# Where the operands of TensorE start within 128 bytes of SBUF: moving them, and joining two pools of slots

## The chip, the core and the metric

The kernel runs on one core of a Trainium2 chip. The metric is the device time of one execution in microseconds (us). Before the change it is 1717.04 us, the median of three runs (1714.14 to 1718.41).

The engines of a core run side by side and in order, each from its own queue: TensorE (PE in the profile; its weight loads stand apart as PEld), VectorE (DVE), ScalarE (ACT), GpSimd (POOL), and SyncE (SP), which here issues every DMA. TensorE reads both operands of a matmul from SBUF: the stationary one is loaded into the array (LDWEIGHTS), then the moving one is streamed through it. Results go to PSUM.

## The reference

Two layers (`DEPTH` 2) over a sequence of 512 rows of width 1024. Each layer projects x, runs four token mixers on 256 columns each, merges them under gates, projects and normalises, and then does a SwiGLU feed-forward network (FFN) of width 2816:

```
for l in range(DEPTH):
    h = x @ w_in[l]
    ...
    o_ret = _retention(rq, rk, rv, rg)
    o_att = _chunk_attention(aq, ak, av, att_rel_bias[l])
    o_gla = _gla(gq, gk, gv, gr, ga, gla_w_a[l], gla_b_a[l])
    o_s5 = _s5(su, ...)
    for bi in range(N_BRANCH):        # summed over the four branches
        gate = sigmoid(x @ w_gate[l, bi] + b_gate[l, bi])
        mixed = mixed + gate * (branches[bi] @ w_branch[l, bi])
    x = _layer_norm(DEEPNORM_ALPHA * x + mixed @ w_out[l], ...)
    ffn = (silu(x @ w_ffn_gate[l]) * (x @ w_ffn_up[l])) @ w_ffn_down[l]
    x = _layer_norm(DEEPNORM_ALPHA * x + ffn, ...)
```

All of it is float32.

## The kernel before

**Numbers.** A float32 operand of a matmul is split into a high part h (ScalarE casts it to float32r) and a low part l (VectorE subtracts h). A product takes three matmuls: h·h, h·l, l·h. So TensorE does three times the plain work, 11,596 matmuls in all, of up to 512 moving columns each.

**What lies where.** x^T stays in SBUF as XH and XL, eight slices of 128 rows by 512 columns each. A tile of weights of 128 by 1024 comes by DMA into `wr` and is split into `wh` and `wl` (`wload`, L312; pool `wp`, three buffers of each). Everything else of 128 by 512 lives in slots (`slot`, L161) of 2048 bytes per partition: 41 of tag "a", 7 of "sg" and 8 of "acc" in the pool `ap`, and 12 of tag "w" in the pool `ap2`. `ap2` lies 64 bytes further than a multiple of the slot's size behind `ap`, because of a tile of 16 floats between them (L148 to L150). A tag's slots are handed out in turn, and a tile waits until the last reader of the slot's former tile is done.

**The stages of a layer.** First come the projections that all branches need (`gemm_n`, tiles gn, with x^T stationary and the weights moving; then su, aq, ak by `gemm_t`, with the weights stationary and x^T moving, 256 columns at a time, tiles of 48 matmuls). Then the mixers run, as generators that `run` (L984) interleaves by the clock of a planner (`Pace`, L51): attention, retention (rq, rk, rg), gla (gq, gr) and s5, and as filler `gate_stream` (L917), which alternates gate tiles (`pg`, 48 matmuls of x^T against w_gate) and branch tiles (`pb`, 6 matmuls of 512 columns, the branch br moving against its weights bw stationary). Then `proj_ln` (L444) multiplies the merged rows (mh, ml, stationary) by w_out (moving, tiles pj) and normalises. The FFN makes 44 tiles `pg` of x^T against w_gate and w_up, and `proj_ln` again multiplies their results (gh, gl, stationary) by w_down (moving, tiles pj). In `proj_ln` all k but the last two take their weights by `wload`; the last two by `wload_s` (L327) into slots `wsh`, `wsl`. Of the 22 tiles gh and gl of the FFN, f = 0 to 6 and 13 to 21 lie in `ap`, f = 7 to 12 in `ap2`.

**The s5 mixer** (L770) works through eight blocks j. A block's input u is fetched by DMA (`skr`), cast by ScalarE to `stk`; its matrix is split into `sbs` (once for two blocks, `split_b`, L778: a cast by ScalarE, a subtraction by VectorE); two matmuls `sv` read both; a chain on VectorE turns them into states (m1 to m4 are named sm); `xr` and `xi` are split from those; six matmuls `sy` take them one block later, against `cpd`. At the end comes `sg`, a small product with `swg`.

**Order.** The calls stand in the order in which the generators run, and the tile framework then orders the instructions of each engine by priority and by its own estimates; when a slot comes free is part of that. On the chip each engine takes its queue strictly in order.

**Where the operands start,** as the built program has them (bytes past a multiple of 128; matmul slices within a tile start at multiples of 512 bytes but for a few of gn):

| tiles | before | after |
|---|---|---|
| XH, XL | 0 | 0 |
| wh, wl (and wr) | 64 | 64 |
| constants ct (identity for transposes) | 0 | 64 |
| slots of `ap`: br, mh, gh (16 of 22), wsh, stk, xr, xi, v, ... | 0 | 64 |
| slots of `ap2`: bw, sbs, cpd, swg, gh (f = 7 to 12) | 64 | 64 (in `ap`) |

Of the kernel before, what the change touches and what calls it, by code (L numbers as in the profile page):

```python
# [10 lines left out]
F32 = mybir.dt.float32  # L11
F32R = mybir.dt.float32r
# [4 lines left out]
P = 128  # L17
S = 512
# [18 lines left out]

BUFS = {"a": 41, "sg": 7, "acc": 8, "w": 12}

# [89 lines left out]
def trunk_kernel(ctx: ExitStack, tc: tile.TileContext, xn, xt, wt, w2, wbr, wo, wgu, wdn,  # L134
# [6 lines left out]
    def pool(name, bufs, **kw):  # L141
        return ctx.enter_context(tc.tile_pool(name=name, bufs=bufs, **kw))

    cp = pool("cp", 1)
    wp = pool("wp", 3)
    sm = pool("sm", 2)
    ap_ = pool("ap", 53)
    pad = pool("pad", 1)  # L148
    ap2 = pool("ap2", 12)
    pad.tile([P, 16], F32, name="pad")  # L150
    psm = pool("psm", 3, space=bass.MemoryType.PSUM)
    psx = pool("psx", 5, space=bass.MemoryType.PSUM)
    dr = pool("dr", 1, space=bass.MemoryType.DRAM)
# [3 lines left out]
    def nm(s):  # L157
        uid[0] += 1
        return f"{s}{uid[0]}"

    def slot(s, dt=F32, tag="a"):  # L161
        n = nm(s)
        return (ap2 if tag == "w" else ap_).tile([P, 512], dt, tag=tag, name=n, bufs=BUFS[tag])

    def mm_ps(s):
        n = nm(s)
        x = psm.tile([P, 512], F32, tag="mm", name=n)
        pace.ring("mm", 3, x)
        return x

    def mx_ps(s):
        n = nm(s)
        x = psx.tile([P, 512], F32, tag="mx", name=n)
        pace.ring("mx", 5, x)
        return x

    def split(h, l, src):
        A.copy(h, src)
        V.tensor_tensor(l, src, h.bitcast(F32), ALU.subtract)

    def split_slots(s, src, tags=("a", "a")):
        h, l = slot(s + "h", F32R, tags[0]), slot(s + "l", F32R, tags[1])
        split(h, l, src)
        return h, l

    def three(pairs):

        (ah, al), (bh, bl) = pairs
        return ((ah, bh), (ah, bl), (al, bh))


    XH = cp.tile([P, 8, S], F32R, name="XH")
    XL = cp.tile([P, 8, S], F32R, name="XL")

    def load_x(k):
        r = slot("xr")
        SP.dma_start(r, xt[:, k, :])
        with tc.high_priority():
            split(XH[:, k, :], XL[:, k, :], r)

# [138 lines left out]
    def gemm_t(src, s, late=None):  # L339

        return gemm_ts([src], s, late)[0]

    def gemm_ts(srcs, s, late=None):
        wl = [wload(x) for x in srcs]
        pss = [mm_ps(s) for _ in srcs]
        for (t0, t1) in ((0, 256), (256, S)):
            for i, ((h, l), ps) in enumerate(zip(wl, pss)):
                if late and t0 == 0 and i == len(wl) - 1:
                    late()
                n = 0  # L350
                for w, xx in ((h, XH), (h, XL), (l, XH)):
                    for k in range(8):
# [5 lines left out]
    def gemm_n(srcs, width, pre=None, late=None):  # L358
# [4 lines left out]
        def prod(c, t):  # L363
            h, l = ws[c]
            for kk in range(2):
                k = 2 * c + kk
                for j, (xx, w) in enumerate(((XH, h), (XL, h), (XH, l))):
                    T.matmul(pss[t][:, :width], xx[:, k, P * t:P * t + P],
# [16 lines left out]
    def layer_norm(l, w_, xh, pss, gt, bt, t, last):  # L385
# [30 lines left out]
        def rest():  # L416
# [15 lines left out]
            for h in range(2):  # L432
                split(XH[:, 4 * h:4 * h + 4, P * t:P * t + P], XL[:, 4 * h:4 * h + 4, P * t:P * t + P],
                      xf[h].rearrange("p (k c) -> p k c", c=P))
# [335 lines left out]
    def s5(l, s5c, uspr, br):  # L770

        bst = {}
# [3 lines left out]
            SP.dma_start(r[0:96, :], sb[l, :, 512 * c:512 * c + 512])  # L776

        def split_b(c):  # L778
            r, b = bst[c], slot("sbs", F32R, "w")
            A.copy(b[0:96, :], r[0:96, :])  # L780
            V.tensor_tensor(b[64:96, :], r[64:96, :], b[64:96, :].bitcast(F32), ALU.subtract)
            bst[c] = b
# [32 lines left out]

        def inputs(j):
            u0, g0 = 32 * (j % 4), j // 4
            cpd = slot("cpd", F32R, "w")
            G.memset(cpd.bitcast(F32), 0.0)
            cp4 = cpd.rearrange("p (s i c) -> p s i c", s=2, i=2)  # L820
            csrc = cc.rearrange("p (i j c) -> p i j c", i=2, c=32)[:, :, j]
            split(cp4[:, 0, :, u0:u0 + 32], cp4[:, 1, :, u0:u0 + 32], csrc)
            vv = []
            u = ust.pop(j)
            for i in range(2):
                ps = mx_ps("sv")
                c0 = 256 * (j % 2) + P * i
                T.matmul(ps, bst[j // 2][0:96, c0:c0 + P], u[0:96, :], start=True, stop=True)
                vv.append(ps)
            er, ei = tabs[j]  # L830
            m1, m2, m3, m4 = (slot("sm") for _ in range(4))
            V.tensor_tensor(m1, vv[0], er, ALU.mult)
            V.tensor_tensor(m4, vv[0], ei, ALU.mult)
            V.tensor_tensor(m2, vv[1], ei, ALU.mult)
            V.tensor_tensor(m3, vv[1], er, ALU.mult)
            V.tensor_tensor(m1, m1, m2, ALU.add)
            V.tensor_tensor(m3, m3, m4, ALU.subtract)
            return cp4, m1, m2, m3, m4
# [40 lines left out]
        for j in range(8 + LAG):  # L879
# [9 lines left out]
            if j == 6:  # L889
                wg = slot("swg")  # L890
# [2 lines left out]
                yield [*xs[j - LAG][1], *xs[j - LAG][2]]  # L893
                outputs(j - LAG)
        yield [wg]
        wgh = split_slots("swg", wg, ("w", "w"))
        yield [*wgh, *yg[0][1], *yg[1][1]]
        for p in range(2):
            ps = mx_ps("sg")
            n = 0  # L900
# [16 lines left out]
    def gate_stream(l, order, brs, mix):  # L917


        sgs, bws, acc = {}, {}, [None] * 8  # L920

        def gate(bi, i):
            pg = gemm_t(wt[l, 13 + 8 * bi + i], "pg")
            sgs[bi, i] = slot("sg", tag="sg")
            A.activation(sgs[bi, i], pg, AF.Tanh, bias=hb[:, l, 8 * bi + i:8 * bi + i + 1], scale=0.5)

        def load(bi, c):
            bws[bi, c] = slot("bwr")
            SP.dma_start(bws[bi, c], wbr[l, bi, c])

        def branch(bi, i, first, last):
            sg = sgs.pop((bi, i))
            pb = mm_ps("pb")
            n = 0
            for k in range(2):
                for a, b in three((bws[bi, i // 2], brs[bi][k])):
                    c0 = 256 * (i % 2) + P * k
                    T.matmul(pb, a[:, c0:c0 + P], b, start=(n == 0), stop=(n == 5))
                    n += 1
            if first:  # L940
                acc[i] = slot("acc", tag="acc")
                V.scalar_tensor_tensor(acc[i], sg, 1.0, pb, ALU.add, ALU.mult)
            else:
                V.scalar_tensor_tensor(sg, sg, 1.0, pb, ALU.add, ALU.mult)
                (V if last else G).tensor_tensor(acc[i], acc[i], sg, ALU.add)
            if last:

                h, l_ = slot("mh", F32R), slot("ml", F32R)
                A.activation(h, acc[i], AF.Copy, scale=0.5)
                V.scalar_tensor_tensor(l_, acc[i], 0.5, h.bitcast(F32), ALU.mult, ALU.subtract)  # L950
                mix.append((h, l_))

        todo = [(bi, i) for bi in order for i in range(8)]
        ng = nb = nl = ns = 0

        def inputs_at():
            x = brs[todo[nb][0]]
            return None if x[0] is None or x[1] is None else pace.ready([*x[0], *x[1]])

        def can():  # L960
            return 0.0 if ng < len(todo) and ng - nb < CAP else inputs_at()

        while nb < len(todo):
            yield can
            at = inputs_at()
            more = ng < len(todo) and ng - nb < CAP
            if ng - nb >= 2 and at is not None and at <= pace.at["T"] or not more:
                branch(*todo[nb], nb < 8, nb >= 24)
                nb += 1
            else:  # L970
                gate(*todo[ng])
                ng += 1

            while ns < min(nl, (nb + 6) // 2):
                c = todo[2 * ns][0], todo[2 * ns][1] // 2
                if pace.when(bws[c]) > pace.at["T"] and ns > nb // 2:
                    break
                bws[c] = split_slots("bw", bws[c], ("w", "w"))
                ns += 1
            while nl < min(len(todo), nb + 6) // 2:  # L980
                load(todo[2 * nl][0], todo[2 * nl][1] // 2)
                nl += 1
# [23 lines left out]
    for l in range(L):  # L1006
# [73 lines left out]
        for f in range(NF):  # L1080
            if f > 0:
                ps += [gemm_t(wgu[l, i], "pg") for i in range(max(3, 2 * f), 2 * f + 2)]
            pg, pu = ps[2 * f:2 * f + 2]
            if f == 1:
                rows()
            s = slot("fs")
            A.activation(s, pg, AF.Silu)
            V.tensor_tensor(s, s, pu, ALU.mult)
            h, l_ = split_slots("g", s, ("acc", "acc") if f < 4 else ("sg", "sg") if f < 7 else
                                ("w", "w") if f < 13 else ("a", "a"))  # L1090
            ghs.append(h)
            gls.append(l_)
            if l + 1 < L and f == 0:
                s5c = s5_constants(l + 1)
            if l + 1 < L and f % 2 == 0 and 4 <= f < 20:
                j = f // 2 - 2
                for i, x in enumerate(s5_table(j, s5c[3])):
                    SP.dma_start(esp[j, i], x)
# [141 lines left out]
```

## Time and profile before

| | |
|---|---|
| time, median of 3 runs | 1717.04 us |
| time of the profiled execution | 1721.47 us |
| its span, first to last instruction | 1719.4 us |
| granted TensorE clock, mean of the span | 0.979 of full speed |
| busy: PE, PEld, DVE, ACT, POOL | 96%, 89%, 59%, 36%, 21% |
| matmuls | 11,596 |

The times below are microseconds from the start of the span. Layer 0 runs its mixers from about 67 to 459, w_out to 487, the FFN to about 858; layer 1 follows with its mixers from 905 to 1299, w_out to 1327, and the FFN to the end. A matmul's own duration in the trace (about 390 ns for 512 columns) is its passage through a pipeline: the next one starts before it ends. What a stream of matmuls costs is read from the distance of their starts. In the timeline equal neighbours are merged: a row gives the start of the first, the time to the end of the last, and their count.

### The profile page before, as it was taken

What the parts mean: (1) busy time and instruction counts of PE and PEld (TensorE: products, weight loads), DVE (VectorE), ACT (ScalarE), POOL (GpSimd) and SP (SyncE); (2) the same over time, 40 slices, a digit from 0 to 9 for tenths busy, and PEclk for the clock granted to TensorE, in tenths of its full rate; (3) what the DMA queues carried; (4) which work ended last, traced back from release to release, by engine and by line L of the source; (5) the groups of instructions that cost most, each with busy time, mean ns of one, the idle gap of its engine ahead of it and who ended that gap; (6) DMA issues with size and microseconds to landing.
All of it is one profiled execution on the core that took longest, in us unless ns stands there. A gap on an engine that the chain in (4) does not pass through costs nothing. (4 is left out here: it accounts for less than half of the span.)

```text
span 1719.4 us, 27810 instructions
## 1 busy us (share of the span) xinstructions
PE 1650.6 (96%) x11596; PEld 1526.8 (89%) x11596; DVE 1005.9 (59%) x1473; ACT 613.0 (36%) x1012; POOL 353.4 (21%) x363
## 2 busy tenths in 40 slices
PE   8998999789999999999999999999899999999997
PEld 7988998679889999998889889988898899999886
DVE  4667579998577443332374765699965833333226
ACT  4443442233343222221253545433332522222112
POOL 0602015642018931000052000121200600000002
PEclk9998999899999999999999999999999999999999
DMA  5522322222432433322317332233424232332232
GB/s 196 179 94 69 96 74 76 88 90 90 141 111 87 123 123 123 123 90 94 122 54 261 116 96 87 75 118 108 139 95 160 86 100 98 99 99 99 98 99 74
DMA packets 66206, 186.94 MB, mean 109 GB/s; under 512 B 7137, under 2 KB 7329, under 8 KB 66081
## 3 DMA queue, kind: packets, MB, share of 16 engines
q1 hardware_dynamic: 66080, 185.17, 33.0%
q8 instruction: 91, 1.49, 0.4%
q14 instruction: 35, 0.28, 0.1%
HBM read 170.46 MB, written 14.68 MB: 108 GB/s over the span
## 5 line engine op out<-in xcount | busy, mean ns | idle before, releaser
L122 DVE TENSOR_TENSOR wl<-wr,wh 128x1024 fp32r<-128x1024 f32 (+2 forms) x250 | 318.3, 1275 | 439.7 <-ACT wh L122 425.4
L122 ACT CAST wh<-wr 128x1024 fp32r<-128x1024 f32 (+2 forms) x250 | 257.6, 1032 | 672.2 <-PE pg L122 221.6
L122 PE MATMUL pg<-XH,wh 128*128 128x256 f32 x2432 | 333.4, 280 | 3.1 <-DVE fs L122 2.2
L122 PE MATMUL pg<-XL,wh 128*128 128x256 f32 x2432 | 331.0, 279 | 2.5 <-DVE XL L122 2.5
L122 PE MATMUL pg<-XH,wl 128*128 128x256 f32 x2432 | 328.8, 278 | 0.0
L122 PEld LDWEIGHTS pg<-XH,wh 128*128 128x128 f32 x2432 | 308.3, 191 | 9.1 <-issue 3.1
L122 PEld LDWEIGHTS pg<-XL,wh 128*128 128x128 f32 x2432 | 303.6, 190 | 3.3 <-DVE XL L122 3.3
L122 PEld LDWEIGHTS pg<-XH,wl 128*128 128x128 f32 x2432 | 302.2, 190 | 0.0
L122 POOL TENSOR_TENSOR rs<-ve,ct 128x1 f32<-128x1 f32 x16 | 10.9, 682 | 715.3 <-DVE ve L122 715.3
L122 DVE TENSOR_TENSOR fs<-fs,pg 128x512 f32<-128x512 f32 x44 | 30.2, 687 | 159.2 <-PE pg L122 159.2
L122 PE MATMUL pj<-wh,gh 128*128 128x512 f32 x320 | 101.9, 392 | 0.0
L122 PE MATMUL pj<-wl,gh 128*128 128x512 f32 x320 | 101.8, 391 | 0.0
L122 PE MATMUL pj<-wh,gl 128*128 128x512 f32 x320 | 101.6, 390 | 0.0
L122 POOL TENSOR_TENSOR acc<-acc,sg 128x512 f32<-128x512 f32 x32 | 54.5, 1704 | 171.2 <-DVE sg L122 163.0
L122 PEld LDWEIGHTS pj<-wl,gh 128*128 128x128 f32 x320 | 60.1, 188 | 12.9
L122 PEld LDWEIGHTS pj<-wh,gl 128*128 128x128 f32 x320 | 60.1, 188 | 12.9
L122 PEld LDWEIGHTS pj<-wh,gh 128*128 128x128 f32 x320 | 59.9, 188 | 12.9
L122 POOL TENSOR_TENSOR hr<-hv,ct 128x8 f32<-128x8 f32 x8 | 13.2, 1648 | 240.4 <-DVE hv L122 240.4
L122 PE MATMUL gn<-wh,XH 128*128 128x400 f32 (+1 forms) x128 | 50.0, 391 | 5.6 <-ACT XH L122 5.5
L122 DVE TENSOR_TENSOR_SCAN sm<-mag,sm 128x512 f32<-128x512 f32 x32 | 52.5, 1677 | 0.0
L122 PE MATMUL pb<-brh,bwh 128*128 128x512 f32 x128 | 52.2, 408 | 0.0
L122 PE MATMUL pb<-brl,bwh 128*128 128x512 f32 x128 | 51.8, 404 | 0.0
(320 smaller groups left out, 2608.4 us busy)
## 6 DMA issues: line engine op xcount, KB each, us to landing
wr<-in_wt SPq DMA_DIRECT2D x90, 512.0 KB
wr<-in_wgu SPq DMA_DIRECT2D x88, 512.0 KB
wr<-in_wdn SPq DMA_DIRECT2D x44, 512.0 KB
bwr<-in_wbr SPq DMA_DIRECT2D x32, 256.0 KB
wr<-in_wo SPq DMA_DIRECT2D x16, 512.0 KB
skr<-spr SPq DMA_DIRECT2D x32, 192.0 KB
wr<-in_w2b SPq DMA_DIRECT2D x8, 400.0 KB
wr<-in_w2a SPq DMA_DIRECT2D x8, 256.0 KB
```

Of the source, the lines that this page charges most:

```text
L122: r = fn(out, *a, **kw)
```

## The change

x^T gets a pool of its own, `xp`, ahead of the constants, and after it and after the constants and the small tiles stands a tile of 16 floats (64 bytes). So x^T stays at a multiple of 128 bytes and the weights, the constants and all slots start 64 bytes past one (the table above). The pool `ap2` and the tag "w" go; its twelve slots join tag "a", which has 53 now.

```
-BUFS = {"a": 41, "sg": 7, "acc": 8, "w": 12}
+BUFS = {"a": 53, "sg": 7, "acc": 8}
...
+    def pad(i, n):
+        pool(f"pad{i}", 1).tile([P, n], F32, name=f"pad{i}")
+
+    xp = pool("xp", 1)
+    pad(0, 16)
     cp = pool("cp", 1)
+    pad(1, 16)
     wp = pool("wp", 3)
     sm = pool("sm", 2)
+    pad(2, 16)
     ap_ = pool("ap", 53)
-    pad = pool("pad", 1)
-    ap2 = pool("ap2", 12)
-    pad.tile([P, 16], F32, name="pad")
...
-        return (ap2 if tag == "w" else ap_).tile([P, 512], dt, tag=tag, name=n, bufs=BUFS[tag])
+        return ap_.tile([P, 512], dt, tag=tag, name=n, bufs=BUFS[tag])
...
-    XH = cp.tile([P, 8, S], F32R, name="XH")
-    XL = cp.tile([P, 8, S], F32R, name="XL")
+    XH = xp.tile([P, 8, S], F32R, name="XH")
+    XL = xp.tile([P, 8, S], F32R, name="XL")
...
-            r, b = bst[c], slot("sbs", F32R, "w")
+            r, b = bst[c], slot("sbs", F32R)
...
-            cpd = slot("cpd", F32R, "w")
+            cpd = slot("cpd", F32R)
...
-        wgh = split_slots("swg", wg, ("w", "w"))
+        wgh = split_slots("swg", wg)
...
-                bws[c] = split_slots("bw", bws[c], ("w", "w"))
+                bws[c] = split_slots("bw", bws[c])
...
-            h, l_ = split_slots("g", s, ("acc", "acc") if f < 4 else ("sg", "sg") if f < 7 else
-                                ("w", "w") if f < 13 else ("a", "a"))
+            h, l_ = split_slots("g", s, ("acc", "acc") if f < 4 else ("sg", "sg") if f < 7 else ("a", "a"))
```

No instruction is added or taken away on the five engines, but some stand elsewhere in their queues, since a tile of former tag "w" now takes its turn among the slots "a": 36 of the matmuls, 52 instructions of ACT, 87 of DVE, 11 of POOL and 8 of SP's DMAs. On TensorE it is mostly the `sv` pairs of s5. This is the last of them in layer 0, before the change:

```order
L122 MATMUL pb788_4380<-brh574_3082,bwh712_3918 128x512
L122 MATMUL pb788_4380<-brl575_3083,bwh712_3918 128x512
L122 MATMUL pb788_4380<-brh574_3082,bwl713_3919 128x512
L122 MATMUL pb788_4380<-brh578_3093,bwh712_3918 128x512
L122 MATMUL pb788_4380<-brl579_3094,bwh712_3918 128x512
L122 MATMUL pb788_4380<-brh578_3093,bwl713_3919 128x512
L122 MATMUL sv791_4395<-stk781_4312,sbs747_4115 128x512
L122 MATMUL sv792_4397<-stk781_4312,sbs747_4115 128x512
L122 MATMUL pg800_4415<-XH_82,wh798_4410 128x256 x8
```

And the same place of TensorE's queue after it (the line numbers are one lower, and the numbers behind the names eight higher):

```order
L121 MATMUL pb788_4388<-brh574_3090,bwh712_3926 128x512
L121 MATMUL pb788_4388<-brl575_3091,bwh712_3926 128x512
L121 MATMUL pb788_4388<-brh574_3090,bwl713_3927 128x512
L121 MATMUL pb788_4388<-brh578_3101,bwh712_3926 128x512
L121 MATMUL pb788_4388<-brl579_3102,bwh712_3926 128x512
L121 MATMUL pb788_4388<-brh578_3101,bwl713_3927 128x512
L121 MATMUL pg800_4423<-XH_90,wh798_4418 128x256 x5
L121 MATMUL sv791_4403<-stk781_4320,sbs747_4123 128x512
L121 MATMUL sv792_4405<-stk781_4320,sbs747_4123 128x512
L121 MATMUL pg800_4423<-XH_90,wh798_4418 128x256 x3
```

Five matmuls of the next gate tile now stand ahead of the pair; the last pair of layer 1 (sv2116) moves by the same five.

On VectorE the subtraction that makes `sbs` moves back in its queue. This is the one for the blocks 6 and 7 of layer 0, before the change (`sv758` is the pair that reads it first):

```order
L122 TENSOR_TENSOR sbs747_4115<-sbr727_4006,sbs747_4115 32x512
L122 TENSOR_TENSOR sm725_3998<-er685_3737,sm726_3999 128x512
L122 TENSOR_TENSOR xrl743_4101<-sm723_3996,xrh742_4100 128x512
L122 TENSOR_TENSOR er685_3737<-ei686_3738,sm724_3997 128x512
L122 SCALAR_TENSOR_TENSOR sg719_3986<-sg719_3986,pb749_4120 128x512
L122 TENSOR_TENSOR sm725_3998<-sm725_3998,er685_3737 128x512
L122 TENSOR_TENSOR cpd757_4197<-scc94_778,cpd757_4197 128x2x32
L122 TENSOR_TENSOR xil745_4105<-sm725_3998,xih744_4104 128x512
L122 TENSOR_TENSOR wl799_4411<-wr797_4409,wh798_4410 128x1024
L122 SCALAR_TENSOR_TENSOR sg739_4086<-sg739_4086,pb755_4186 128x512
L122 TENSOR_TENSOR sm760_4205<-sv758_4201,er729_4010 128x512
```

And after it:

```order
L121 TENSOR_TENSOR sm725_4006<-er685_3745,sm726_4007 128x512
L121 TENSOR_TENSOR xrl743_4109<-sm723_4004,xrh742_4108 128x512
L121 TENSOR_TENSOR er685_3745<-ei686_3746,sm724_4005 128x512
L121 TENSOR_TENSOR wl799_4419<-wr797_4417,wh798_4418 128x1024
L121 TENSOR_TENSOR sm725_4006<-sm725_4006,er685_3745 128x512
L121 SCALAR_TENSOR_TENSOR sg739_4094<-sg739_4094,pb755_4194 128x512
L121 TENSOR_TENSOR xil745_4113<-sm725_4006,xih744_4112 128x512
L121 TENSOR_TENSOR sbs747_4123<-sbr727_4014,sbs747_4123 32x512
L121 TENSOR_TENSOR cpd757_4205<-scc94_786,cpd757_4205 128x2x32
L121 TENSOR_TENSOR sm760_4213<-sv758_4209,er729_4018 128x512
```

The subtraction stands behind xil745 now, the last but one before the first reader of the new `sv`. The other `sbs` that follow a running chain (for the blocks 2 and 4 of both layers and 6 of layer 1) move back by five to eight places in the same way.

## Rows read from the trace of the kernel before

**Rows 1.** The page, busy time and share of the span: TensorE.

```profile
PE 1650.6 (96%) x11596; PEld 1526.8 (89%) x11596; DVE 1005.9 (59%) x1473; ACT 613.0 (36%) x1012; POOL 353.4 (21%) x363
```

**Rows 2.** Stretches: us, busy time of each engine (count), clock, DMA.

```profile
230.00:403.50 173.50, 149.47 (x1065) 138.88 (x1063) 157.75 (x192) 52.96 (x85) 87.37 (x61) 0.93 0.26 84
403.50:459.00 55.50, 55.48 (x411) 52.16 (x412) 41.31 (x58) 23.67 (x34) 1.29 (x1) 1.00 0.24 81
...
1299.00:1327.00 28.00, 28.00 (x124) 22.92 (x123) 12.12 (x16) 7.64 (x10) 0.00 (x0) 1.00 0.70 231
1589.00:1693.50 104.50, 104.50 (x462) 86.01 (x461) 27.13 (x26) 21.39 (x23) 0.00 (x0) 1.00 0.27 91
```

**Rows 3.** Waits of TensorE: who for whom, us in total, times, longest.

```profile
PE sv L122 <- ACT stk L122: 33.8, 11, 6.7
```

**Rows 4.** Timeline of TensorE in the FFN's w_down, layer 0: start, us.

```profile
764.49 0.62 PE L122 MATMUL pj<-wh,gh 128*128 128x512 f32 x2
...
786.46 0.62 PE L122 MATMUL pj<-wh,gh 128*128 128x512 f32 x2
...
797.42 0.61 PE L122 MATMUL pj<-wh,gh 128*128 128x512 f32 x2
...
824.62 0.62 PE L122 MATMUL pj<-wh,gh 128*128 128x512 f32 x2
```

**Rows 5.** The same timeline where the weights lie in slots.

```profile
856.22 0.40 PE L122 MATMUL pj<-wsh,gh 128*128 128x512 f32 x1
...
857.61 0.40 PE L122 MATMUL pj<-wh,gh 128*128 128x512 f32 x1
```

**Rows 6.** The chain that ended last, 1240 to 1300: start, us, what.

```profile
1251.09 10.88 PE pg L122 x96
...
1274.25 2.79 PE sg L122 x12
...
1282.49 8.39 PE pb L122 x36
```

**Rows 7.** Groups of TensorE by shape: busy us, mean ns, idle before.

```profile
L122 PE MATMUL pj<-wh,gh 128*128 128x512 f32 x320 | 101.9, 392 | 0.0
...
L122 PE MATMUL pb<-brh,bwh 128*128 128x512 f32 x128 | 52.2, 408 | 0.0
...
L122 PE MATMUL pj<-wsh,gh 128*128 128x512 f32 x32 | 12.7, 396 | 0.0
```

**Rows 8.** Timeline at the last sv of layer 0 and of layer 1.

```profile
402.85 0.61 ACT L122 CAST stk<-skr 96x512 fp32r<-96x512 f32 x1
...
403.52 0.73 PE L122 MATMUL sv<-stk,sbs 96*128 96x512 f32 x2 [2.30 <-ACT stk L122]
...
1241.91 1.19 PE L122 MATMUL sv<-stk,sbs 96*128 96x512 f32 x2 [2.12 <-ACT stk L122]
```

**Rows 9.** Timeline of TensorE: matmuls that stream x^T.

```profile
67.95 1.11 PE L122 MATMUL rq<-XL,wh 128*128 128x256 f32 x8
...
313.60 1.11 PE L122 MATMUL pg<-XH,wh 128*128 128x256 f32 x8
...
319.26 0.39 PE L122 MATMUL sy<-xrh,cpd 128*128 128x512 f32 x1
...
1151.28 1.10 PE L122 MATMUL pg<-XH,wh 128*128 128x256 f32 x8
```

**Rows 10.** Timeline of TensorE from the tiles gn into su, layer 1.

```profile
899.69 0.40 PE L122 MATMUL gn<-wl,XH 128*128 128x512 f32 x1
...
903.57 0.62 PE L122 MATMUL su<-XL,wh 128*128 128x256 f32 x4
```

**Rows 11.** Timeline at the third block of s5, layer 0, and the next wait.

```profile
285.80 1.76 DVE L122 TENSOR_TENSOR xil<-sm,xih 128x512 fp32r<-128x512 f32 x1
...
286.34 0.73 PE L122 MATMUL sv<-stk,sbs 96*128 96x512 f32 x2 [1.88 <-ACT stk L122]
...
310.05 1.22 PE L122 MATMUL sv<-stk,sbs 96*128 96x512 f32 x2 [6.74 <-ACT stk L122]
```

## The prediction

> **What bounds the kernel.** I read the busy times first, then the stretches, then TensorE's waits, and last its timeline at matmul level. TensorE is busy for 1650.6 of 1719.4 us [rows 1], so what counts is either the pace of its stream or one of its gaps. The stretches say where which of the two holds [rows 2]. In w_out (1299 to 1327) and w_down (1589 to 1693.5) it is busy for every microsecond, at full clock: there a matmul that costs 1 ns less shortens the kernel by 1 ns. In the s5 part of the mixers (230 to 403.5 in layer 0) it is busy for 149.5 of 173.5 us, beside a VectorE that is busy for 157.8: there TensorE stops at the pairs `sv`, which wait for `stk` from ACT, 33.8 us in 11 waits [rows 3], and ACT's cast stands behind casts that wait for VectorE's chain. After the last `sv` (403.5 to 459) TensorE is full again, 55.48 of 55.50.
>
> The pace depends on where operands start. In w_down of layer 0 the tiles with weights at 64 and gh at 0 run from 764.49 to 786.46, four k of 24 matmuls: 21.97/96 = 228.9 ns apart. Those with weights at 64 and gh at 64 (f = 7 to 12, the slots of `ap2`) run from 797.42 to 824.62, five k: 27.20/120 = 226.7 ns [rows 4]. Same loop, same engines beside it, same clock; what differs is the place of gh. With weights and gh both at 0 (`wsh`) six matmuls take 856.22 to 857.61, 231.7 ns each [rows 5]. With br, or the states, moving at 0 against weights at 64 the chain has 36 pb in 8.39 us, 233.1 ns, and 12 sg in 2.79, 232.5 [rows 6]. The gate tiles have x^T moving at 0 against weights at 64, too, but with 256 columns: 96 in 10.88 us, 113.3 ns [rows 6], which is 226.7 for 512. So both at 64 is the fastest pair that is to be seen for 512 columns, and x^T against weights at 64 already has that pace. The change brings all other pairs to 64 and 64, and leaves that of x^T alone.
>
> **Part by part.**
>
> (a) w_out and w_down, weights by `wload`. Of three products with gh, 320 matmuls each [rows 7], 96 are at 64 and 64 already, so 3 x 224 = 672 change; for mh, six of eight k have such weights: 6 x 24 x 2 layers = 288. 960 x (228.9 - 226.7) = 2.1 us, all on the path [rows 2].
>
> (b) The last two k of each, weights in slots: 32 in each of six groups [rows 7], 192. They go from 0 and 0 to 64 and 64: 192 x (231.7 - 226.7) = 0.95 us. Bounds: 0 to 0.95, since both operands move together, and if only their distance counts, nothing changes. I take it whole, because the one row for 64 and 64 has no slow stretch.
>
> (c) pb, sg and sy behind the last `sv`: per layer 48 + 12 + 12 = 72, 144 in all, x (233.1 - 226.7) = 0.9 us, on the path.
>
> (d) pb and sy ahead of the last `sv`: of 384 pb [rows 7] 288, of 96 sy 72, 360 x 6.4 = 2.3 us, and some 0.9 in the attention, retention and gla products (0 and 0 before, about 200 of them at the 5.0 of (b)). Here TensorE arrives earlier at a pair `sv` that is released by ACT and VectorE, and waits longer: the last one still has 2.30 us of wait in layer 0 and 2.12 in layer 1 [rows 8]. Between 0 and 3.2 us; I take a quarter, 0.8, for the stretches ahead of the first long waits.
>
> (e) The order. The last pair of each layer stands five gate matmuls later; its release does not depend on them (stk ends at 403.46 [rows 8], and TensorE stood idle). So 5 x 113.3 ns of work move from behind the wait into it: 0.57 us a layer, 1.1 us. The `sbs` subtraction is later on VectorE. At the third block of layer 0 the pair is released by `stk` at 286.3; now it waits for a subtraction behind xil, which ends at 287.56, and one more operation: about 288.2 to 288.9, so 1.9 to 2.6 us later [rows 11]. Queued behind that pair on TensorE are pb and gate tiles, and nobody but the next `sv` waits for them in earnest: that one waits for 6.74 us at 310.05 anyway [rows 11], so the loss ends there. I cost it at nothing; without that cover it is at most 3 such moves x 2 layers x 2.6 = 16 us, and with the last wait as a second cover only what exceeds 2.1 us in a layer would show. The tiles bw are split later too, but the first pb reads them long after.
>
> (f) x^T against weights: 152 gate and FFN tiles of 48. The pair stays as it is, and the sum takes 0. But this stream has two paces. From 313.60 to 319.26 a gate tile takes 5.66/48 = 117.9 ns per matmul [rows 9], 4.6 more than in rows 6, with the same addresses. In the timeline some sixteen tiles do that, from 67.95 to 1151.28 [rows 9], and each time it is the whole tile: the stream stays at the pace at which it starts. Which one that is hangs on what runs ahead of it, and that does change. Nearest row for an x^T stream that follows moving operands at 64: gn into su, 899.69; from 899.93 on 32 matmuls take 3.64 us to 903.57, 113.8 ns, so it settles at the fast pace [rows 10]. Bounds: -3.5 us (16 x 48 x 4.6, all slow tiles gone, most of it ahead of waits) to +19 us (the 88 FFN tiles x 48 x 4.6).
>
> Sum: 2.1 + 0.95 + 0.9 + 0.8 + 1.1 = 5.9 us. The profiled execution took 1721.47, so 1715.6 on its terms; it was 4.4 above the median of the runs, 1717.04, so the time to expect is 1711.1.
>
> **A rule that speaks against it.** Rows 4 show 2.2 ns between two places of the same operand. The Trainium skill ("SBUF — State Buffer", section "A bandwidth-pool intuition that's wrong (but worth ruling out)") has TensorE read the moving operand and the weights through two independent ports, and knows contention only as a lock or a starved descriptor writer. By that rule the place of an operand costs nothing and (a) to (d) are 0; the trace differs by 2.2 to 6.4 ns a matmul. It is the first rival below.
>
> **Rivals.**
>
> No change. The two paces of rows 4 come from something that goes along with f = 7 to 12, such as the slot's higher address, not from the 64 bytes; or what 0 and 0 costs, 64 and 64 costs too (rows 4 have it for one loop only). Then only (e) is left: 1716, and with the later `sbs` 1715 to 1719. For it: 0 and 0 has the same distance and is the slower one. Against it: the fast stretch begins and ends with f = 7 and 13 and has no slow matmul in between.
>
> More. All of (d) reaches the end, and the slow x^T tiles vanish, since the 233 ns streams that they follow are gone: 5.9 + 2.4 + 2 to 3.5 = about 11, 1706. Against it: the waits of rows 8 swallow most.
>
> Slower. The x^T stream starts at the slow pace where it started at the fast one, behind pb, sy and transposes whose addresses all move. Place: the FFN, whose streams are the longest. Both layers: 88 x 48 x 4.6 = 19 us, 1730; one: 1721. It decides from 5.9/(48 x 4.6 ns) = 27 tiles on. For it: the same addresses have shown both paces. Against it: rows 10, and both FFN streams are fast now, each after several interruptions.
>
> **How the numbers follow.** Forecast, 1708 to 1715: 0.50. No change: 0.22. More: 0.10. Slower: 0.18. I say 1711.1. The range 1704 to 1721 takes in "more", "no change" and one FFN at the slow pace, and leaves out both FFNs. What this measurement tells from no change is about 0.3%, 5.2 us, so faster means under 1711.9: 0.65 of the forecast, all of "more", a bit of the rest, 0.45. Slower means over 1722.2: two thirds of "slower" and some of "no change" by a late `sbs`, 0.16. Within: 0.39.
>
> **What would show it.** The timeline of w_down at 226.7 ns for all k, `wsh` included; 36 pb of the last branch in 8.16 us; TensorE's waits for `sv` as long as before or longer, at the third block by some 2 us; x^T tiles of 5.44 us. I am wrong if pb or `wsh` stay at 231 to 233, or if an x^T stream of the FFN shows 118 ns.

## The result: 1740 us, slower by 1.1%

The changed kernel takes 1739.99 us (median of 6 runs, 1730.41 to 1741.57), the kernel before, measured beside it, 1717.72 (6 runs, 1711.79 to 1726.17). The ratio is 1.0109, with a 95% interval of 1.0077 to 1.0140. The forecast was 1711.1 with a range to 1721: it had the wrong sign.

The page of the kernel after shows TensorE busy for 23.1 us more [rows 1], in a span of 1738.8 us:

```profile
PE 1673.7 (96%) x11596; PEld 1556.3 (90%) x11596; DVE 999.9 (58%) x1473; ACT 613.6 (35%) x1012; POOL 353.5 (20%) x363
```

Cut at the first and the last matmul `pj` of each w_out and w_down, the two profiled spans differ like this (us). So cut, the stages end later than the times given ahead of the prediction: before has the last `pj` of layer 0's w_out at 504.7 and that of its w_down at 875.8.

| stage | before | after | difference |
|---|---|---|---|
| start to the first `su` | 32.0 | 32.7 | +0.7 |
| mixers, layer 0 | 426.9 | 429.0 | +2.1 |
| w_out, layer 0 | 45.7 | 45.2 | -0.5 |
| gate and up tiles of the FFN, layer 0 | 248.8 | 255.7 | +6.9 |
| w_down, layer 0 | 122.3 | 121.3 | -1.0 |
| mixers, layer 1, with the norm ahead | 423.2 | 427.1 | +3.9 |
| w_out, layer 1 | 45.7 | 45.1 | -0.6 |
| gate and up tiles, layer 1 | 244.7 | 253.7 | +9.0 |
| w_down, layer 1, and the end | 130.0 | 129.1 | -0.9 |

Where the weights are the moving operand, the forecast came true: -3.1 us in the four w_out and w_down. Where x^T is the moving operand, it did not. These are two stretches of 200 us inside the gate and up tiles of the FFN, one in layer 0 and one in layer 1, TensorE alone (columns: stretch, us, PE busy with the count of matmuls, granted clock, DMA share, GB/s), first of before:

```profile
540.00:740.00 200.00, 200.00 (x1767) 1.00 0.38 120
1380.00:1580.00 200.00, 200.00 (x1767) 1.00 0.30 98
```

and of after:

```profile
540.00:740.00 200.00, 200.00 (x1700) 1.00 0.36 119
1380.00:1580.00 200.00, 200.00 (x1701) 1.00 0.29 95
```

TensorE is never idle in them, at the full of its two clocks (2.4 GHz), and yet fewer matmuls fit: 200/1767 = 113.2 ns each before, 200/1700 = 117.6 after. Such a row reads a pace without any timeline, and I use them, mostly the second, for the kernels below.

The slow pace is everywhere in after, not in the FFN alone. Counted start to start over all 8544 matmuls that stream 256 columns of x^T, before has 7463 at 112 to 114 ns and 858 at 115 to 120; after has 329 and 7982. Those 7124 at 4.5 ns are 32 us of TensorE's time: 4182 of them, 18.8 us, in the two FFNs, and 2940, 13.2 us, in the mixers. The table shows 15.9 and 6.

In the FFN of layer 0 the clock hides a part. Both kernels stop there for `fs` (2.21 us before, 1.79 after). In before the clock fell to the lower of TensorE's two levels (1.2 GHz) a microsecond behind that stop and stayed there for 3.4 us; after kept 2.4 GHz. The whole stage and that stretch in before (columns as above):

```profile
504.60:753.40 248.80, 244.32 (x2131) 0.99 0.37 117
535.40:538.80 3.40, 3.40 (x19) 0.50 0.55 169
```

and the stage in after:

```profile
506.90:762.60 255.70, 251.90 (x2131) 1.00 0.34 114
```

Run 4 below has the fast pace without that drop, and this stage took it 247.2 us, 1.6 less than before. So the slow pace costs 8.5 us in layer 0 (255.7 - 247.2) and 9.0 in layer 1, 17.5 in both. In the mixers TensorE has waits for `sv` that can take up a part, and their mean granted clock differs too (0.95 before and 0.96 after in layer 0); how the 13.2 us divide between the two is not shown.

Even `su` behind `gn`, my nearest row [rows 10], is slow now:

```profile
908.17 0.40 PE L121 MATMUL gn<-wl,XH 128*128 128x512 f32 x1
908.40 1.10 PE L121 MATMUL su<-XH,wh 128*128 128x256 f32 x8
909.35 1.10 PE L121 MATMUL su<-XL,wh 128*128 128x256 f32 x8
910.29 1.10 PE L121 MATMUL su<-XH,wl 128*128 128x256 f32 x8
```

16 matmuls from 908.40 to 910.29, 118.1 ns each, where 113.8 stood.

The chain of layer 1 (start, us, what) shows the gate tiles slower and the branch tiles faster, side by side; it answers to [rows 6]:

```profile
1262.03 11.31 PE pg L121 x96
...
1286.04 2.75 PE sg L121 x12
1288.78 5.66 PE pg L121 x48
1294.44 8.20 PE pb L121 x36
```

96 pg take 11.31 (10.88 before), 36 pb 8.20 (8.39), 12 sg 2.75 (2.79). In the timeline of w_down the tiles with f = 0 to 6 go at the pace that only f = 7 to 12 had [rows 4], and the shared weights too [rows 5]:

```profile
765.30 0.62 PE L121 MATMUL pj<-wh,gh 128*128 128x512 f32 x2
...
792.50 0.62 PE L121 MATMUL pj<-wh,gh 128*128 128x512 f32 x2
...
865.26 0.39 PE L121 MATMUL pj<-wsh,gh 128*128 128x512 f32 x1
...
867.30 0.39 PE L121 MATMUL pj<-wsh,gh 128*128 128x512 f32 x1
```

120 matmuls in 27.20 us and nine in 2.04: 226.7 ns both times.

**What had moved.** My table of addresses was taken modulo 128. There x^T is at 0 and the weights at 64 in both kernels. But the change puts a pad of 64 bytes behind x^T and another ahead of the weights, and both lie between the two: the weights moved by 128 bytes against x^T. Modulo 256, as the built programs have it:

| | x^T | weights | slots | weights minus x^T |
|---|---|---|---|---|
| before | 128 | 192 | 128, and 192 in `ap2` | 64 |
| after | 128 | 64 | 64 | 192 |

By distance I mean, from here on, the start of the stationary operand minus that of the moving one, modulo 256. For x^T that is the last column. In w_down the weights move and gh stands: there it was 192 before (228.9 ns), 0 for f = 7 to 12 (226.7 ns), and is 0 everywhere in after. For pb it was 64 (233.1 ns) and is 0.

### The profile page after: what moved, and what is told of

Read it like the earlier page. It is cut to its first block, busy times and chain, and to the rows that moved or that the text cites. A ratio compares the mean times of both kernels' runs of the same rounds, so it can differ in the third digit from the quotient of the medians.

```text
span 1738.8 us, 27806 instructions
## 1 busy us (share of the span) xinstructions
PE 1673.7 (96%) x11596; PEld 1556.3 (90%) x11596; DVE 999.9 (58%) x1473; ACT 613.6 (35%) x1012; POOL 353.5 (20%) x363
## 5 line engine op out<-in xcount | busy, mean ns | idle before, releaser
L121 PE MATMUL pg<-XH,wh 128*128 128x256 f32 x2432 | 345.2, 284 | 1.8 <-DVE fs L121 1.8
L121 PE MATMUL pg<-XL,wh 128*128 128x256 f32 x2432 | 339.8, 281 | 2.3 <-DVE XL L121 2.3
L121 PE MATMUL pg<-XH,wl 128*128 128x256 f32 x2432 | 338.5, 281 | 0.0
L121 PEld LDWEIGHTS pg<-XH,wh 128*128 128x128 f32 x2432 | 318.8, 192 | 7.7 <-issue 2.7
L121 PEld LDWEIGHTS pg<-XL,wh 128*128 128x128 f32 x2432 | 311.5, 190 | 3.1 <-DVE XL L121 3.1
L121 PEld LDWEIGHTS pg<-XH,wl 128*128 128x128 f32 x2432 | 310.6, 189 | 0.2
L121 POOL TENSOR_TENSOR acc<-acc,sg 128x512 f32<-128x512 f32 x32 | 61.7, 1929 | 169.4 <-DVE sg L121 169.4
L121 POOL TENSOR_TENSOR hr<-hv,ct 128x8 f32<-128x8 f32 x8 | 13.2, 1648 | 192.9 <-DVE hv L121 192.9
L121 PE MATMUL pb<-brh,bwl 128*128 128x512 f32 x128 | 51.2, 400 | 0.0
```

What stands on the lines that cost most here:

```text
L121: r = fn(out, *a, **kw)
```

## The experiments

Every ratio below is against the kernel before as it was measured beside those runs (medians 1720.49 us for runs 1 to 4, 1714.73 for 5 to 8, 1717.15 for 9 to 12).

Three theories. **D**: the distance of weights from x^T modulo 256 sets the pace of an x^T stream; 64 allows the fast one, 192 does not. **S**: the streams ahead (pb, sy, sg, transposes), whose operands all moved, hand their pace over; this is the rival "slower" of the prediction. **W**: it is the place of the weights alone.

**1. Distance 64 again, all else as in the change.**

```
-    pad(1, 16)
+    pad(1, 48)
```

> The changed kernel with 128 bytes more between the constants and the weights, so that the weights wh, wl and all slots lie 192 bytes past a multiple of 256 instead of 64, and x^T at 128 as in both kernels: the distance from x^T to the weights, taken modulo 256, is 64 again as before the change (192 in the changed kernel). Theory D (the distance modulo 256 sets the pace of the x^T stream): gate and FFN tiles at 113.3 ns per matmul again, all pairs of slots and weights at 226.7 ns, about 1709 us, some 30 under the changed kernel. Theory S (the streams that run ahead, whose operands are all at 64 past 128 now, set the pace): tiles stay at 117.8 ns, 1740 us. Theory W (the place of the weights alone, modulo 256, sets it: 192 fast, 64 slow): as D here, 1709.

Measured: 1725.39 us (10 runs, 1713.97 to 1731.19), ratio 0.9992 [0.9961, 1.0024]. The loss is gone in the mean, but the two FFNs of the profiled execution differ:

```profile
540.00:740.00 200.00, 200.00 (x1700) 1.00 0.37 119
1380.00:1580.00 200.00, 200.00 (x1768) 1.00 0.31 98
```

and the chain shows slow gate tiles behind even branch tiles (I call a stream of 512 columns even where every matmul starts 226 or 227 ns behind the last; at distance 64 it is 231 and 236 in turn):

```profile
1293.78 8.16 PE pb L121 x36
1301.93 5.65 PE pg L121 x48
```

So the distance of 64 brings the fast pace back, but only as one of two. 4354 of the x^T matmuls are still slow in this execution, which was the slowest of the ten.

**2. The kernel before, with its weights, and the slots behind them, moved by 128 bytes.**

```
     cp = pool("cp", 1)
+    padw = pool("padw", 1)      # with one tile of 32 floats
     wp = pool("wp", 3)
```

> The kernel before with 128 bytes put between the constants and the weights and nothing else: weights at 64 past a multiple of 256 (192 before), x^T at 128, slots shifted by 128 too, the pairs of slots and weights as before modulo 128, the order of instructions as before. Theory D: distance 192, x^T tiles at 117.8 ns, 1718 + about 30 = 1745 to 1750 us. Theory S: the streams ahead are as before, so 113.3 ns and 1718. Theory W: weights at 64, slow, 1745 to 1750.

Measured: 1739.98 us (4 runs, 1739.22 to 1742.91), ratio 1.0100 [1.0071, 1.0129]. Order, slots and the places of pb's operands relative to each other are those of before; the FFNs are those of after:

```profile
540.00:740.00 200.00, 200.00 (x1700) 1.00 0.37 119
1380.00:1580.00 200.00, 200.00 (x1700) 1.00 0.29 96
```

and so are the gate tiles, while pb keeps the pace of before:

```profile
1286.83 5.65 PE pg L122 x48
1292.49 8.39 PE pb L122 x36
```

That is a loss as large as the whole one, by one move of 128 bytes; neither the new order nor the joined pool nor another stream ahead is needed for it.

**3. All at the other places, distance 192 kept** (the changed kernel with x^T at 0 and weights and slots at 192: a tile of 32 floats ahead of `xp`).

> The changed kernel with everything 128 bytes further on: x^T at 0 past a multiple of 256, weights and slots at 192, so the distance stays 192. Theory D: slow as the changed kernel, 1740 us, tiles at 117.8 ns. Theory W: weights at 192, fast, 113.3 ns, 1709. Theory S: 1740.

Measured: 1737.14 us (4 runs, 1734.49 to 1740.91), ratio 1.0082 [1.0050, 1.0114], 8015 slow x^T matmuls.

```profile
1380.00:1580.00 200.00, 200.00 (x1701) 1.00 0.30 96
```

The weights lie where they lay before, and the loss is there: W falls.

**4. The same with weights and slots at 64, distance 64** (`pad(1, 48)` added).

> The changed kernel with x^T 128 bytes further on and weights and slots 256 bytes further on: x^T at 0 past a multiple of 256, weights and slots at 64, distance 64. Theory D: fast, 113.3 ns, 1709 us. Theory W: weights at 64, slow, 117.8 ns, 1740. Theory S: 1740.

Measured: 1723.37 us (10 runs, 1712.75 to 1736.30), ratio 1.0009 [0.9976, 1.0043].

```profile
540.00:740.00 200.00, 200.00 (x1767) 1.00 0.38 122
1380.00:1580.00 200.00, 200.00 (x1767) 1.00 0.30 98
```

The weights lie where after has them, and the FFN is fast; 2430 x^T matmuls are slow, nearly all in the mixers. This execution was the fastest of its ten. Together, 1 to 4 show D for these two distances: in the profiled executions of before and of all runs at distance 64 (1, 4, 5, 9 and 10) the FFN was fast in 10 of 12 layers, at 192 (after, runs 2 and 3) in none of 6. It is no strict rule: 329 x^T matmuls of after are fast at 192. S remains as a second effect at distance 64.

**5. The joined pool alone** (before with 53 slots in `ap` and no pads; x^T and weights as before).

> The kernel before with its slots joined in one pool, and nothing of the shifts: x^T at 128 and the weights at 192 modulo 256 as before, all slots at 128 (sbs, cpd, the shared gate's and bw's second part were at 192). Theory D (the distance weights minus x^T modulo 256 sets the pace of the x^T streams; 64 here): no large loss, 1715 to 1724. Theory S (a stream takes the pace of the one ahead of it; where pb, sg and sy go at an even 226.7 ns the gate tile behind starts slow): these pairs do not come to 226.7 ns here, so the gate tiles keep their paces of before and the time is that of before within 0.3%. A third theory, O (the new order from the joined pool costs time by itself): slower than before by 0.5% or more.

Measured: 1726.84 us (6 runs, 1719.58 to 1729.49), ratio 1.0062 [1.0041, 1.0083]. By the number that is O's. The profiled execution took 1721.59, against 1721.47 for before, with mixers of 426.4 and 424.0 us (426.9 and 423.2). That does not refute O: before's profiled execution was a long one (beside run 5 it took 1710.74 to 1718.04), and its mixers ran at a mean granted clock of 0.95 and 0.98, those of run 5 at 0.96 and 0.99. What the trace shows is S: 2443 x^T matmuls are slow (858 before), and the gate tiles behind pb and sg are among them.

```profile
1276.82 5.65 PE pg L122 x48
1282.47 8.19 PE pb L122 x36
1290.65 5.65 PE pg L122 x48
```

My expectation under S was wrong, since I held pb at 128 and 128 for uneven; it is even (8.19/36 = 227.5). The 1585 more slow matmuls are 7.1 us of TensorE's time in the mixers; whether they or the order make up the 0.6% stays open.

**6 to 8. The distances 128 and 0.** Run 6 has the first pad ahead of x^T (x^T 192, the rest 64). Run 7 is the same with `pad(1, 48)` (all at 192). Run 8 is the changed kernel with `pad(1, 32)` (all at 128).

> The changed kernel with the first 64 bytes of padding ahead of x^T instead of behind it: x^T at 192 modulo 256, weights and slots at 64, distance 128. Neither theory has a row for this distance of x^T. D1 (only the distance of 192 is slow): 1710 to 1722. D2 (any distance but 64 and 0 is slow): 1735 to 1742 as the changed kernel. S alone: as the changed kernel's twin at distance 64, 1714 to 1731, with gate tiles behind pb and sy slow.

> The same with 128 bytes more ahead of the weights: x^T, weights and slots all at 192 modulo 256, distance 0. Theory D: the w_down matmuls of the changed kernel have weights and gh at the same place modulo 256, and all go at 226.7 ns, so x^T at distance 0 goes at 113.3 ns from any entry: before's 1717.7 less 3.9 us (w_out, w_down, wsh, the last pb) less 858 slow x^T matmuls of before at 4.45 ns = 3.8 us: 1710, with no slow x^T tile. Theory S: a gate tile behind an even pb or sy starts slow and stays slow, 1714 to 1731.

> The changed kernel with 64 bytes more ahead of the weights: x^T, weights and slots all at 128 modulo 256, distance 0 again, but on multiples of 128. Theory D by the distance alone: as with all at 192, 1710. Theory M (two streams that both lie on multiples of 128 are slower by themselves, as wsh at 231.7 ns was before): w_out, w_down and wsh 5.0 ns longer than in the changed kernel on 1152 matmuls = 5.8 us more, and x^T half of that each on 8544 = 21 us more than at 113.3 ns: 1735 to 1742.

Measured: 1745.57, 1754.10 and 1749.35 us (4 runs each), ratios 1.0182 [1.0154, 1.0209], 1.0231 [1.0210, 1.0253], 1.0202 [1.0183, 1.0222]. The stretch of layer 1 for 6:

```profile
1380.00:1580.00 200.00, 200.00 (x1688) 1.00 0.29 96
```

and for 8:

```profile
1380.00:1580.00 200.00, 200.00 (x1669) 1.00 0.29 94
```

So 128 gives 118.5 ns (D2) and 0 gives 119.8, the slowest of all, in 7 and 8 alike: 1710 was far off. I had carried the best distance of w_down (512 columns move) over to x^T (256 move). In the same two kernels (7 and 8) w_down is as fast as in after, 121.3 and 119.5 us from its first `pj` to its last. The best distance differs with the shape, and multiples of 128 are not slow as such: M falls too, for w_down and for the shared weights, which go at 226.7 ns with everything at 128 (six matmuls, 1.36 us):

```profile
874.73 0.39 PE L121 MATMUL pj<-wsh,gh 128*128 128x512 f32 x1
...
876.09 0.39 PE L121 MATMUL pj<-wh,gh 128*128 128x512 f32 x1
```

In run 5 the same pair, both at 128, takes 1.39 us for six:

```profile
864.54 0.40 PE L122 MATMUL pj<-wsh,gh 128*128 128x512 f32 x1
...
865.93 0.40 PE L122 MATMUL pj<-wh,gh 128*128 128x512 f32 x1
```

There the k ahead of it has weights at 192 against gh at 128 and is uneven. I read this as the pair going on in the pace that it finds: its own places are the same in both runs.

**9 and 10. Distance 64 for x^T, and w_down at distance 0, with pb as before.** Run 9 is before with 64 bytes ahead of `ap`, in the order of before, instruction for instruction. Run 10 also takes all of gh into `ap` (45 slots there, 8 in `ap2`).

> The kernel before with 64 bytes of padding ahead of the slots and nothing else; the order is that of before, x^T at 128 and weights at 192 modulo 256 as before (distance 64), the slots of the large pool now at 192 and the twelve others at 0. So w_down and the shared weights come to distance 0 for gh 0 to 6 and 13 to 21 and for mh, and to 64 for gh 7 to 12; pb, sy and sg keep their distance of 64 between the two operands. Theory D with S (at distance 64 an x^T stream takes the pace that the stream ahead hands it, and pb, sy and sg at distance 64 end on 231 or 236 ns as before): the gate tiles keep their paces of before, some 860 slow x^T matmuls; w_down gains 960 x 2.4 = 2.3 us and the shared weights 192 x 4.6 = 0.9, and the 288 of gh 7 to 12 lose 6 ns each = 1.7: 1.5 us faster than before, a ratio of 0.999. Rival E (what made the gate tiles of the runs at distance 64 slow was the even w_down, or the slots at 64 past a multiple of 128 in themselves, not pb's distance): some 4000 slow x^T matmuls as where all slots were together, a ratio of 1.000 to 1.010.

> The same, with all of gh in the large pool (45 slots, 8 in the other), so that every w_down pair has distance 0 while pb, sy and sg keep 64. The order shifts by this on all engines. D with S: against the twin with gh 7 to 12 apart 288 x 6 ns = 1.7 us less, 3.2 us less than before, a ratio of 0.998 if the order costs nothing. Rival E: 1.000 to 1.010 with some 4000 slow x^T matmuls.

Measured: 1719.76 us (12 runs, 1713.30 to 1728.68), ratio 1.0008 [0.9983, 1.0033], and 1717.13 (12 runs, 1708.07 to 1727.56), ratio 0.9990 [0.9965, 1.0015]. Neither interval tells the 1.5 or 3.2 us from nothing. Run 10's w_out and w_down took 331.1 us in all, from first to last `pj` (331.0 in after, 334.2 before), so that gain came. In run 9 the tiles with f = 7 to 12 have distance 64 in w_down, and go at 233.3 ns, where the same tiles went at 226.7 (distance 0) before. Slow x^T matmuls: 1829 and 3929, more than the 860 that I expected, so E is not refuted by the count and stays open. The timeline of run 10 shows what goes along with the pace of a tile. These are two gate tiles (start, us; eight matmuls a row), each behind its last pb:

```profile
1135.68 0.40 PE L122 MATMUL pb<-brh,bwl 128*128 128x512 f32 x1
1135.92 1.09 PE L122 MATMUL pg<-XH,wh 128*128 128x256 f32 x8
...
1137.75 1.07 PE L122 MATMUL pg<-XH,wl 128*128 128x256 f32 x8
...
1140.47 1.07 PE L122 MATMUL pg<-XH,wl 128*128 128x256 f32 x8
...
1143.02 0.39 PE L122 MATMUL pb<-brh,bwl 128*128 128x512 f32 x1
1143.25 1.10 PE L122 MATMUL pg<-XH,wh 128*128 128x256 f32 x8
...
1145.13 1.11 PE L122 MATMUL pg<-XH,wl 128*128 128x256 f32 x8
...
1147.96 1.11 PE L122 MATMUL pg<-XH,wl 128*128 128x256 f32 x8
```

The first goes at (1140.47 - 1137.75)/24 = 113.3 ns, the next at (1147.96 - 1145.13)/24 = 117.9, with the same places. From the start of the last pb to that of the tile the trace has 236 ns in the one and 229 in the other. Over all kernels at distance 64 (before and runs 1, 4, 5, 9, 10), gate tiles of 48 matmuls in one piece right behind a 512-column matmul of 232 to 245 ns (from its start to the tile's) were fast, 66 of 66; behind one of 225 to 231 ns 122 of 134 were slow. Another 40, behind shorter or longer ones, went 24 fast and 16 slow. At distance 192 (after, runs 2 and 3) 27 of 30 were slow even behind 232 to 245. So at 64 the pace goes along with how the stream ahead ends, as S has it, and at 192 there is little left to decide; no run sets the length of that last matmul by itself.

A stop can decide, too, and for longer. In layer 0 of run 10 the FFN waits once for `fs`; from there on 1919 matmuls are slow, up to its end, 8.5 us:

```profile
529.16 1.18 PE L122 MATMUL pg<-XH,wh 128*128 128x256 f32 x8 [2.22 <-DVE fs L122]
530.18 1.11 PE L122 MATMUL pg<-XL,wh 128*128 128x256 f32 x8
```

Before has the same wait, and ends up fast:

```profile
534.15 1.18 PE L122 MATMUL pg<-XH,wh 128*128 128x256 f32 x8 [2.21 <-DVE fs L122]
...
539.53 1.07 PE L122 MATMUL pg<-XL,wh 128*128 128x256 f32 x8
540.44 1.07 PE L122 MATMUL pg<-XH,wl 128*128 128x256 f32 x8
```

The two differ in the clock: the rows left out in before are those of its 3.4 us at 1.2 GHz (535.40 to 538.80, above), and run 10 stays at 2.4. But the drop does not decide. Of the six kernels at distance 64, before, 5 and 9 have it and go on fast, run 1 has it and goes on slow; run 4 has none and goes on fast, run 10 none and slow. What decides at the stop stays open.

In layer 1 of run 10 the stream stays fast (x1768 in the second stretch). The runs of one kernel at distance 64 spread over 7 to 24 us, those of after, 2 and 3, at 192, over 11, 4 and 6; steps of 8.5 us a layer would do the larger ones, but only the profiled executions have a trace.

**11 and 12. Distances 96 and 32** (the changed kernel with `pad(1, 56)` and `pad(1, 40)`).

> The changed kernel with the weights and slots 160 bytes further on: x^T at 128, weights and slots at 224 modulo 256, distance 96. The pace so far by distance: 0 at 120.0 ns, 64 at 113.3 or 117.8, 128 at 119.0, 192 at 117.8. Theory F (the pace follows the distance in steps finer than 64): a pace between, 113 to 119 in another share; G (only the 64-byte line counts, so 96 is as 64): 113.3 and 117.8 mixed, 1714 to 1731.

> The same at a distance of 32: weights and slots at 160 modulo 256. F: its own pace, 1714 to 1755. G (as distance 0, the line of 64 bytes that it starts in): 120.0 ns for each x^T matmul, 1747 to 1755.

Measured (4 runs each): 1739.15 us, ratio 1.0115 [1.0080, 1.0150], and 1743.45, ratio 1.0139 [1.0098, 1.0180]; the stretch of layer 1 for 96:

```profile
1380.00:1580.00 200.00, 200.00 (x1707) 1.00 0.29 96
```

and for 32:

```profile
1380.00:1580.00 200.00, 200.00 (x1692) 1.00 0.30 96
```

F: each has a pace of its own, and G falls. At 32, 96 and 128 it is a mean: the starts there follow each other at 115 to 124 ns in a cycle that repeats. The table for 256 columns of x^T, in ns per matmul, from these rows:

| distance modulo 256 | 0 | 32 | 64 | 96 | 128 | 192 |
|---|---|---|---|---|---|---|
| pace | 119.8 | 118.2 | 113.2 or 117.6 | 117.2 | 118.5 | 117.6 |

None of the twelve beats the kernel before by more than the measurement can tell.

## Why the prediction was wrong

- **The step that failed** is (f): "The pair stays as it is, and the sum takes 0." It did not stay: 64 became 192 modulo 256. I had compared addresses modulo 128 and never asked whether 128 was the period; no row of before could show that it was not, since it has x^T at one distance only. So the term that the sum took at 0 was 32 us of TensorE's time, and 17.5 us of the two FFNs. Run 2 makes this move without the new order and the joined pool, and takes 1739.98 us.
- **The idea behind (a) to (c)**, that "both at 64" is the fast place, was wrong, and its numbers were right. What counts is the distance of the two operands, which the change brings to 0; runs 7 and 8 have the same w_down at 192 and at 128. (a) and (b) came to 3.1 us where 3.05 was forecast. That (b) came is luck: the distance of its pairs is 0 before and after, and by its own bound nothing should have changed. Its rows were no evidence on the place 0: the 231.7 ns were most likely handed over by the k ahead (runs 5 and 8). (c) came to 8.20 us for the last 36 pb against 8.16 forecast.
- **(d) and (e).** The wait at the third block of layer 0 is for `sbs` now, as forecast, and the next one covers it [rows 11]. It grew from 1.88 to 3.13 us, but not because the pair is released later, as (e) had it: the pair starts at 284.73, ahead of the 286.34 of before. TensorE came to it 2.9 us earlier, at 281.60, after a mean granted clock of 0.98 in place of 0.96 since the first `su`:

```profile
284.73 0.70 PE L121 MATMUL sv<-stk,sbs 96*128 96x512 f32 x2 [3.13 <-DVE sbs L121]
308.59 1.22 PE L121 MATMUL sv<-stk,sbs 96*128 96x512 f32 x2 [6.18 <-ACT stk L121]
```

  TensorE's waits for `sv` are 18.4 us for `stk`, 13.2 for `sbs` and 0.8 for `bwh` in after, 32.4 in place of 33.8 [rows 3]: a little shorter, where the prediction had them as long or longer. Whether the 2.8 us of (c) to (e) reached the end is not settled: run 2, with the same slow gate tiles and the order of before, has mixers that are 2.9 us shorter than those of after (853.2 and 856.1 in the two layers), so in these two executions they did not.
- **The rival "slower"** had the right place, the right sign and about the right price (19 us for both FFNs; 17.5 came at equal clock, 15.9 as measured, and 6 in the mixers), but the wrong cause. It let the hand-over decide, and gave it 0.18 because rows 10 and both FFNs were fast; at distance 192 neither came again. The hand-over goes with the slow tiles at distance 64, and is the likely reason why run 1, with the distance put right, gains nothing over before; by how much is not shown.
- **The rule weighed.** Rows 4 and the table above have the pace hang on where two operands lie. The Trainium skill ("SBUF — State Buffer", "A bandwidth-pool intuition that's wrong (but worth ruling out)") counts the read for the weights as a second, independent port beside that for the moving operand. From this I took that a move of 128 bytes costs nothing. Run 2 measures 1.0%, so for these float32r streams the measurement decides against that reading. That the moving read and the weight load disturb each other would fit; no run here separates the two, and the mechanism stays open.

## What to carry to other kernels

Where TensorE is full, read its pace as the count of matmuls in a stretch that is busy throughout, and compare kernels by it. When operands are moved in SBUF, write down the distance of every moving and stationary pair modulo at least 256 bytes, before and after, and for each shape apart; a pad is shared by everything behind it, so check the pair that was not meant to move. The distance that was best for one shape here (0 for 512 columns) was the worst for the other (0 for 256). And where runs of one kernel spread, one profiled execution is one draw: compare the clock of a stage before its time.

## What the runs showed of the hardware that was not expected

- A stream of float32r matmuls has several steady paces at the same clock: for 256 columns 113.2 to 119.8 ns by the distance modulo 256 of its operands, for 512 columns 226.7 (distance 0), 228.9 (192) and about 233 (64).
- At distance 64 two paces are possible, 113.2 and 117.6 ns, and the stream keeps the one in which it starts: 48 matmuls of a gate tile, or 1919 of an FFN. For gate tiles the length of the last matmul ahead, 229 or 236 ns, nearly always told which; for an FFN behind a stop nothing here did.
